# Attention keys split once per head, and the low half of the logits multiplied over 64 partitions

## The chip, the cores and the metric

The kernel runs on one core of one Trainium2 chip. The metric is the device time of one execution in microseconds, lower is better. Several runs were timed; one further execution was profiled.

## The reference

A two-layer encoder. Each layer projects the normed input (512 positions, 1024 channels), runs a differential attention of 4 heads beside a long-convolution branch, gates both and projects back. The part that the change touches, cut to what is computed:

```python
q, k: (B, S=512, ATTN_HEADS=4, 2, ATTN_QK_DIM=64)
logits = jnp.einsum('bhcqd,bhckd->bhcqk', q_blk, kt)          # contraction over 64
p = jax.nn.softmax(logits + bias[None, :, None], axis=-1)
w = p[:, :, 0] - lam * p[:, :, 1]                              # two components per head
o = jnp.einsum('bhqk,bhkd->bhqd', w, vt)
```

So every head has two components c = 0, 1, each with 64 key and query channels, and every block of 128 query rows needs one 128 x 512 logits product per component.

## The kernel before, in words

All products are made of two-part numbers: a value is split into a rounded high part and the remainder (`split`, L207 on ScalarE and L208 on VectorE), and a product is high x high + high x low + low x high, three matmuls (`mm3`, L192). Weights come in by DMA as `wraw`, are split into `whi` and `wlo`, and a dense projection of 128 channels is 24 matmuls of 128 x 128 x 512 into a PSUM tile `pd`.

One layer is a long list of steps. In the stretch around the change, `layer` mixes three lists: the 16 attention row blocks (4 heads x 4 blocks, `head_rows`, `head_av`, `head_out`), the dense projections of the next head or of the convolution branch, and in layer 0 also pieces of the filter computation. `mix` spreads them evenly; the tile scheduler then orders the instructions of each engine by priority and its own readiness estimate, so an edit in one step can shift others. In the trace the stretch with the logits lies from about 60 to 182 us (layer 0) and from 555 to 655 us (layer 1).

For one head, `head_proj` has steps q, k and z. Step q (L602, L603) builds two tiles, one per component: the 64 rows of component c hold the high half of the queries, the other 64 rows hold the low half of the same queries. Step k (L607 to L615) builds for each component two key tiles of 128 rows. `kh` holds the high half of the component's 64 key rows, twice: on rows 0 to 63 and on rows 64 to 127 (two ScalarE copies, L612). `kl` holds the low half (VectorE, L614) on the component's own rows and zeros (GpSimd memset, L613) on the other rows. A head's two pairs take two buffers of the pool `s1`.

`head_rows` then does per component two matmuls at L640, both with the same stationary operand, the 128-row query tile. The first, against `kh`, gives (q high + q low) x k high in one pass; the second, against `kl`, gives q high x k low, with the q low rows meeting zeros. VectorE adds the position bias and takes the row extreme (L643), ScalarE takes the exponential (L645), and VectorE combines the components (L650, L651). `head_av` transposes the weights (L659), and `head_out` multiplies by the values (L192 into `po`).

Of the kernel before, what the change touches and what calls it, by code (L numbers as in the profile page):

```python
# [10 lines left out]
F32 = mybir.dt.float32  # L11
F32R = mybir.dt.float32r
AF = mybir.ActivationFunctionType
ALU = mybir.AluOpType
# [108 lines left out]
def tiles(t):  # L123

    return t.rearrange("p (a c) -> p a c", a=4)
# [9 lines left out]
def ahead(n):  # L135

    def wrap(f):
        def g(self, *args):
            with self.tc.high_priority(offset=n):
                return f(self, *args)  # L140
        return g
    return wrap
# [3 lines left out]
class Net:  # L146
# [442 lines left out]
    def head_proj(self, l, h):  # L589


        nc = self.nc
        st = {}

        def q():
            ps = self.proj(l, QC + h * P)
            st["q"] = self.two_of("s1", F32R)
            for c in range(2):
                r, n = slice(c * 64, c * 64 + 64), slice(64 - c * 64, 128 - c * 64)
                q2 = st["q"][c]  # L600
                hi, lo, src = tiles(q2[r]), tiles(q2[n]), tiles(ps[r])[:, :, ::-1]
                nc.scalar.activation(out=hi, in_=src, func=AF.Copy, scale=-0.125)  # L602
                nc.vector.scalar_tensor_tensor(out=lo, in0=src, scalar=-0.125, in1=hi.bitcast(F32), op0=ALU.mult, op1=ALU.subtract)  # L603

        def k():
            ps = self.proj(l, KC + h * P)
            st["k"] = []  # L607
            for c in range(2):
                r, n = slice(c * 64, c * 64 + 64), slice(64 - c * 64, 128 - c * 64)
                kh, kl = self.two_of("s1", F32R)  # L610
                for d in (r, n):
                    nc.scalar.copy(out=kh[d], in_=ps[r])  # L612
                nc.gpsimd.memset(kl[n].bitcast(F32), 0.0)  # L613
                nc.vector.tensor_tensor(out=kl[r], in0=ps[r], in1=kh[r].bitcast(F32), op=ALU.subtract)  # L614
                st["k"].append((kh, kl))  # L615

        def z():
            ps = self.proj(l, ZAC + h * P)
            st["za"] = self.t("za")
            self.silu2(ps, st["za"])  # L620

        return st, [q, k, z]

    @ahead(20)
    def head_rows(self, l, h, i, st):


        nc = self.nc
        if i == 0:
            st["B"] = self.t("ld")  # L630
            t = self.tab[h:h + 1, :]
            self.load(st["B"][:, :896], bass.AP(tensor=t.tensor, offset=t.offset + 1, ap=[[1, P], [1, 896]]))
            st["s"] = self.small(8, "s")
        tsl = slice(i * P, (i + 1) * P)
        s0, s1 = (st["s"][:, 4 * c + i:4 * c + i + 1] for c in range(2))
        p = []
        for c in range(2):
            ps = self.ps("pq")
            for n in range(2):
                nc.tensor.matmul(ps, lhsT=st["q"][c][:, tsl], rhs=st["k"][c][n], start=(n == 0), stop=(n == 1))  # L640
            lg = self.t("a")
            m = self.small(1, f"m{c}")
            nc.vector.tensor_tensor_reduce(out=lg, in0=ps, in1=st["B"][:, 384 - i * P:896 - i * P], scale=1.0, scalar=3e38,  # L643
                                           op0=ALU.add, op1=ALU.min, accum_out=m)
            nc.scalar.activation(out=lg, in_=lg, func=AF.Exp, scale=-1.0, bias=m, accum_out=(s0, s1)[c])  # L645
            p.append(lg)
        r = self.small(1, "r")
        nc.vector.reciprocal(out=r, in_=s1)
        n1 = self.small(1, "n1")
        nc.vector.scalar_tensor_tensor(out=n1, in0=r, scalar=self.nlam[:, l:l + 1], in1=s0, op0=ALU.mult, op1=ALU.mult)  # L650
        nc.vector.scalar_tensor_tensor(out=p[0], in0=p[1], scalar=n1, in1=p[0], op0=ALU.mult, op1=ALU.add)  # L651
        st[i] = p[0]
# [434 lines left out]
```

## Time and profile before

| | |
|---|---|
| median of 3 runs | 963.67 us (961.45 to 964.77) |
| the profiled execution, its own time | 964.15 us |
| span of that execution, first to last instruction | 962.3 us |
| TensorE busy in it | 917.5 us (95%) |
| VectorE, ScalarE, GpSimd busy | 733.4 us (76%), 467.8 us (49%), 39.5 us (4%) |
| mean granted TensorE clock | 0.991 of full speed |

The profile separates TensorE into PE (matmuls) and PEld (loads of the stationary operand, which overlap matmuls). A matmul's recorded end is modelled and overlaps the next one's start, so the distance from start to start is what a matmul costs in a stream, not its recorded duration.

### The profile page before, as it was taken

The page shows a single profiled execution, that of the slowest core. Times are in us where ns is not written, and L with a number is a line of the kernel's source. Part 1 is how long each engine was busy: PE and PEld are TensorE (multiplying, and loading weights), DVE is VectorE, ACT ScalarE, POOL GpSimd, SP SyncE. Part 2 cuts the span into 40 slices and gives each one's busy share as a digit, 9 for nine tenths or more (in the row PEclk, how much of TensorE's full clock was granted, in tenths as well). Part 3 has the DMA queues.
Part 4 walks back from the last instruction along what each step waited for, and adds up shares of the span by engine and source line. Part 5 has one row for each costly group of instructions (what it writes and reads, how often), then busy time and mean ns, then how long its engine had stood idle before and what let it go on. Part 6 is the DMA issues. An engine that isn't in the chain of part 4 may idle for free.

```text
span 962.3 us, 13082 instructions
## 1 busy us (share of the span) xinstructions
PE 917.5 (95%) x4563; PEld 762.0 (79%) x4563; DVE 733.4 (76%) x1415; ACT 467.8 (49%) x889; POOL 39.5 (4%) x58
## 2 busy tenths in 40 slices
PE   5999998999999989999999999999999998999996
PEld 4777777888788878887787878888888887888885
DVE  5679889889889878888647478886788988854623
ACT  5467766554444333565444366664443532333521
POOL 2000000001000000000002000000000000000000
PEclk9999999999999999999999999999999999999999
DMA  6532342443543434244654322333333634233512
GB/s 218 152 115 60 105 129 84 144 122 88 153 120 109 134 109 131 77 145 130 218 176 151 87 81 80 96 89 119 100 107 103 197 112 130 67 98 99 166 53 89
DMA packets 141544, 114.12 MB, mean 119 GB/s; under 512 B 7106, under 2 KB 122464, under 8 KB 141477
## 3 DMA queue, kind: packets, MB, share of 16 engines
q1 hardware_dynamic: 140901, 111.31, 38.7%
q0 software_dynamic: 576, 1.97, 0.7%
q8 instruction: 36, 0.59, 0.3%
q14 instruction: 31, 0.25, 0.1%
HBM read 98.26 MB, written 14.99 MB: 118 GB/s over the span
## 4 chain that ended last, share of the span: by engine, by line
PE 42%; DVE 6%; DMA 2%; ACT 1%; POOL 1%; issue 0%; DVEq 0%; POOLq 0%; ACTq 0%; SPq 0%
PE pd L192 29%; PE po L192 4%; PE pq L192 4%; DMA wraw<-in_w_in 2%; PE pq L640 2%; PE po L204 1%; PE pq L204 1%; PE pt L659 1%; DVE s L961 1%; DVE cx L825 1%; DVE cx L828 0%; DVE yh L936 0%; DVE ld L961 0%; DVE cx L829 0%; POOL rout L226 0%
## 5 line engine op out<-in xcount | busy, mean ns | idle before, releaser
L192 PE MATMUL pd<-hT,whi 128*128 128x512 f32 x1408 | 453.0, 395 | 4.6 <-ACT a L889 2.6
L192 PEld LDWEIGHTS pd<-hT,whi 128*128 128x128 f32 x1408 | 260.7, 188 | 57.5 <-ACT a L889 3.4
L192 PE MATMUL pd<-hT,wlo 128*128 128x512 f32 x704 | 277.6, 394 | 1.9 <-DVE wlo L208 1.8
L207 ACT CAST whi<-wraw 128x512 fp32r<-128x512 f32 x216 | 133.8, 620 | 225.8 <-PE pd L192 116.4
L208 DVE TENSOR_TENSOR wlo<-wraw,whi 128x512 fp32r<-128x512 f32 x216 | 146.4, 687 | 63.7 <-ACT whi L207 62.9
L192 PEld LDWEIGHTS pd<-hT,wlo 128*128 128x128 f32 x704 | 132.4, 188 | 29.7 <-DVE wlo L208 3.1
L645 ACT ACTIVATE a<-a,m 128x512 f32<-128x512 f32 x64 | 46.1, 721 | 20.7 <-DVE m L643 20.4
L643 DVE CUSTOM_DVE_ANT_0 a<-pq,ld 128x512 f32<-128x512 f32 x64 | 43.3, 686 | 4.1 <-PE pq L640 3.3
L640 PE MATMUL pq<-s,s 128*128 128x512 f32 x128 | 46.3, 408 | 0.1
L192 PE MATMUL pd<-ya,whi 128*128 128x512 f32 x128 | 41.7, 393 | 0.0
L724 DVE SCALAR_TENSOR_TENSOR u<-pd,vec,u 128x256 f32<-128x256 f32 (+2 forms) x80 | 39.2, 530 | 2.5 <-ACT u L722 2.3
L192 PE MATMUL pd<-yh,whi 128*128 128x512 f32 x128 | 39.8, 390 | 0.0
L204 PE MATMUL po<-s,fh 128*128 128x256 f32 x160 | 32.4, 302 | 4.4 <-ACT s L207 2.0
L207 ACT CAST s<-cx 128x1024 fp32r<-128x1024 f32 x24 | 25.2, 1050 | 22.9 <-DVE cx L834 20.3
L204 PE MATMUL pq<-s,fh 128*128 128x256 f32 x160 | 35.2, 291 | 0.0
L204 PEld LDWEIGHTS po<-s,fh 128*128 128x128 f32 x160 | 26.9, 206 | 6.8 <-ACT s L207 2.9
L192 PE MATMUL po<-s,yh 128*128 128x256 f32 x192 | 29.3, 287 | 2.1 <-DVE n L650 1.4
L192 PEld LDWEIGHTS po<-s,yh 128*128 128x128 f32 x192 | 26.4, 191 | 5.4 <-ACT s L207 2.1
L208 DVE TENSOR_TENSOR s<-cx,s 128x1024 fp32r<-128x1024 f32 x24 | 29.3, 1222 | 0.6 <-ACT s L207 0.5
L204 PEld LDWEIGHTS pq<-s,fh 128*128 128x128 f32 x160 | 26.8, 189 | 3.2 <-DVE b L437 0.9
L640 PEld LDWEIGHTS pq<-s,s 128*128 128x128 f32 x128 | 23.6, 193 | 5.3 <-issue 0.9
L192 PEld LDWEIGHTS pd<-yh,whi 128*128 128x128 f32 x128 | 23.9, 188 | 4.8
(240 smaller groups left out, 1563.3 us busy)
## 6 DMA issues: line engine op xcount, KB each, us to landing
wraw<-in_w_in SPq DMA_DIRECT2D x192, 256.0 KB
H<-b SPq DMA_DIRECT2D x40, 256.0 KB
ld<-H SPq DMA_DIRECT2D x16, 512.0 KB
wraw<-in_w_out SPq DMA_DIRECT2D x32, 256.0 KB
wraw<-in_w_pa SPq DMA_DIRECT2D x16, 256.0 KB
wraw<-in_w_ph SPq DMA_DIRECT2D x16, 256.0 KB
ld<-tab SPq DMA_DIRECT2D x8, 448.0 KB
yh<-in_x SPq DMA_DIRECT2D x4, 512.0 KB
```

Of the source, the lines that this page charges most:

```text
L192: self.nc.tensor.matmul(out, lhsT=l, rhs=r, start=(first and i == 0), stop=(last and i == n - 1))
L204: self.nc.tensor.matmul(out, lhsT=b, rhs=y, start=(i == 0), stop=(i == len(ops) - 1))
L207: self.nc.scalar.copy(out=hi, in_=src)
L208: self.nc.vector.tensor_tensor(out=lo, in0=src, in1=hi.bitcast(F32), op=ALU.subtract)
L640: nc.tensor.matmul(ps, lhsT=st["q"][c][:, tsl], rhs=st["k"][c][n], start=(n == 0), stop=(n == 1))
L643: nc.vector.tensor_tensor_reduce(out=lg, in0=ps, in1=st["B"][:, 384 - i * P:896 - i * P], scale=1.0, scalar=3e38, op0=ALU.add, op1=ALU.min ...
L645: nc.scalar.activation(out=lg, in_=lg, func=AF.Exp, scale=-1.0, bias=m, accum_out=(s0, s1)[c])
L659: nc.tensor.transpose(out=ps[:, k], in_=w[:, k * P:(k + 1) * P], identity=self.ident)
L724: nc.vector.scalar_tensor_tensor(out=o, in0=src, scalar=w[j], in1=o, op0=ALU.mult, op1=ALU.add)
L825: nc.vector.tensor_tensor(out=X[:, 2 * s:2 * s + 2], in0=U[0], in1=odd, op=op)
L961: nc.vector.scalar_tensor_tensor(out=xt[:, cs], in0=st["o"][tt][:, cs], scalar=r, in1=xt[:, cs], op0=ALU.mult, op1=ALU.add)
```

## The change

In step k, one `split` over all 128 partitions makes the high half (`both`) and the low half (`kl`) of both components at once; the two memsets and the two 64-row subtractions go. `both` is only used to form `kl`; the doubled high tiles are still copied from PSUM, 4 copies of 64 rows, into one more buffer, so that a head again takes two buffers for its keys. In `head_rows` the second matmul of a component takes only the component's own 64 rows of the query tile and of `kl`.

```diff
         def k():
             ps = self.proj(l, KC + h * P)
-            st["k"] = []
+            both, kl = self.two_of("s1", F32R)
+            self.split(both, kl, ps)
+            kh = self.two_of("s1", F32R)
             for c in range(2):
-                r, n = slice(c * 64, c * 64 + 64), slice(64 - c * 64, 128 - c * 64)
-                kh, kl = self.two_of("s1", F32R)
-                for d in (r, n):
-                    nc.scalar.copy(out=kh[d], in_=ps[r])
-                nc.gpsimd.memset(kl[n].bitcast(F32), 0.0)
-                nc.vector.tensor_tensor(out=kl[r], in0=ps[r], in1=kh[r].bitcast(F32), op=ALU.subtract)
-                st["k"].append((kh, kl))
+                r = slice(c * 64, c * 64 + 64)
+                for d in range(2):
+                    nc.scalar.copy(out=kh[c][d * 64:d * 64 + 64], in_=ps[r])
+            st["k"] = kh, kl
...
-            for n in range(2):
-                nc.tensor.matmul(ps, lhsT=st["q"][c][:, tsl], rhs=st["k"][c][n], start=(n == 0), stop=(n == 1))
+            kh, kl = st["k"]
+            r = slice(c * 64, c * 64 + 64)
+            nc.tensor.matmul(ps, lhsT=st["q"][c][:, tsl], rhs=kh[c], start=True, stop=False)
+            nc.tensor.matmul(ps, lhsT=st["q"][c][r, tsl], rhs=kl[r], start=False, stop=True)
```

The change also moves instructions. On TensorE, at the second row block of the first head of layer 1, the row order before was as follows. L640 is the logits product (`s_5580` the queries, `s_5622` and `s_5627` the key tiles of the two components), L192 the dense projection beside it.

```order
L640 MATMUL pq<-s_5622,s_5580 128x512
L192 MATMUL pd<-hT,wlo 128x512
L640 MATMUL pq<-s_5622,s_5580 128x512
L192 MATMUL pd<-hT,whi 128x512 x2
L192 MATMUL pd<-hT,wlo 128x512
L640 MATMUL pq<-s_5627,s_5580 128x512
L192 MATMUL pd<-hT,whi 128x512
L640 MATMUL pq<-s_5627,s_5580 128x512
```

At the same place the order now is this one, with L640 the 128-row product (`s_5617` the two high tiles), L641 the 64-row one (`s_5614` the common low tile) and `s_5572` the queries.

```order
L640 MATMUL pq<-s_5617,s_5572 128x512
L192 MATMUL pd<-hT,wlo 128x512
L641 MATMUL pq<-s_5614,s_5572 128x512
L192 MATMUL pd<-hT,whi 128x512 x2
L192 MATMUL pd<-hT,wlo 128x512
L640 MATMUL pq<-s_5617,s_5572 128x512
L192 MATMUL pd<-hT,whi 128x512
L641 MATMUL pq<-s_5614,s_5572 128x512
```

Nothing moved here; each 64-row product simply stands between two 128-row ones. Over the whole program there are 64 L641, none of them next to another.

On ScalarE, in step k of that same head, the rows before were these (`s_5580` again the queries):

```order
L602 ACTIVATE s_5580<-pd 64x512 x2
L207 CAST whi<-wraw 128x512 x2
L612 CAST s_5622<-pd 64x512 x2
L612 CAST s_5627<-pd 64x512 x2
L207 CAST whi<-wraw 128x512
L645 ACTIVATE a,s<-a,m_5679 128x512
```

and now they are these, where line numbers from the logits on are one higher:

```order
L602 ACTIVATE s_5572<-pd 64x512 x2
L207 CAST whi<-wraw 128x512 x2
L207 CAST s_5614<-pd 128x512
L613 CAST s_5617<-pd 64x512 x4
L207 CAST whi<-wraw 128x512
L646 ACTIVATE a,s<-a,m_5669 128x512
```

One 128-row copy has come in ahead of the four 64-row copies. In layer 0, where the filter pieces are mixed in, the order of all engines shifts more widely; in layer 1 it stays close to what it was.

## Rows read from the trace of the kernel before

**Rows 1.** The page's busy time, share of span and instructions of each engine.
```profile
PE 917.5 (95%) x4563; PEld 762.0 (79%) x4563; DVE 733.4 (76%) x1415; ACT 467.8 (49%) x889; POOL 39.5 (4%) x58
```

**Rows 2.** Busy time of each engine in the two stretches with the logits.
```profile
core 0: us, PE busy (x) PEld busy (x) DVE busy (x) ACT busy (x) POOL busy (x), PEclk, DMA share, GB/s
55.00:183.00 128.00, 120.46 (x615) 97.74 (x614) 112.14 (x259) 86.86 (x177) 6.53 (x9) 0.99 0.34 100
...
555.00:656.00 101.00, 100.92 (x517) 84.91 (x517) 81.17 (x185) 64.95 (x137) 5.64 (x7) 1.00 0.29 85
```

**Rows 3.** Pieces of the chain that ended last: start, us, engine, line, matmuls.
```profile
475.87 5.44 PE po L192 x24
...
647.84 2.05 PE pd L192 x9
```

**Rows 4.** Both products of the logits, L640: ns min/median/max, first and last start.
```profile
L640 PEld LDWEIGHTS pq<-s,s x128: 186/188/338, 59.9 to 655.0; 128*128 128x128 f32 x128
L640 PE MATMUL pq<-s,s x128: 387/391/775, 60.2 to 655.2; 128*128 128x512 f32 x128
```

**Rows 5.** PE around the one product over 33 rows: start, us, shapes, count.
```profile
29.16 0.40 PE L192 MATMUL pd<-wlo,hT 128*128 128x512 f32 x1
29.48 1.12 PE L349 MATMUL pq<-u 33*128 33x512 f32 x2
30.54 0.73 PE L192 MATMUL pd<-whi,hT 128*128 128x512 f32 x2
31.11 0.40 PE L192 MATMUL pd<-wlo,hT 128*128 128x512 f32 x1
```

**Rows 6.** Weight loads at the same place, in brackets the idle time before.
```profile
28.93 0.19 PEld L192 LDWEIGHTS pd<-wlo,hT 128*128 128x128 f32 x1
29.48 0.29 PEld L349 LDWEIGHTS pq<-u 33*128 33x128 f32 x2 [0.36 <-issue]
30.53 0.30 PEld L192 LDWEIGHTS pd<-whi,hT 128*128 128x128 f32 x2 [0.76 <-DVE hT L208]
```

**Rows 7.** PE around the products over 32 rows and 4 columns.
```profile
53.83 0.39 PE L192 MATMUL pd<-hT,wlo 128*128 128x512 f32 x1
54.15 1.88 PE L309 MATMUL pt<-s,rb 32*4 32x512 f32 x4
55.95 0.73 PE L192 MATMUL pd<-hT,whi 128*128 128x512 f32 x2
56.52 0.40 PE L192 MATMUL pd<-hT,wlo 128*128 128x512 f32 x1
```

**Rows 8.** PE around the same kind of product as rows 5, over 128 rows.
```profile
58.13 0.39 PE L192 MATMUL pd<-hT,whi 128*128 128x512 f32 x1
58.36 1.04 PE L349 MATMUL pq<-u 128*128 128x512 f32 x2
58.84 0.79 PE L192 MATMUL pd<-hT,whi 128*128 128x512 f32 x1
59.47 0.39 PE L192 MATMUL pd<-hT,wlo 128*128 128x512 f32 x1
```

**Rows 9.** PE around a product with 128 rows and 4 columns.
```profile
117.84 0.39 PE L192 MATMUL pd<-hT,wlo 128*128 128x512 f32 x1
118.07 0.27 PE L698 MATMUL po<-ident,ro 128*4 128x128 f32 x1
118.18 0.38 PE L659 MATMUL pt<-ident,a 128*128 128x128 f32 x2
```

**Rows 10.** The instructions of step k: ns min/median/max, first and last start.
```profile
L612 ACT CAST s<-pd x32: 566/581/587, 54.7 to 627.3; 64x512 fp32r<-64x512 f32 x32
L613 POOL MEMSET s<- x16: 518/522/530, 22.0 to 605.9; 64x512 f32 x16
L614 DVE TENSOR_TENSOR s<-pd,s x16: 674/688/696, 56.0 to 628.0; 64x512 fp32r<-64x512 f32 x16
```

**Rows 11.** Splits of 128 rows on ScalarE and VectorE, from the page's costliest groups.
```profile
L207 ACT CAST whi<-wraw 128x512 fp32r<-128x512 f32 x216 | 133.8, 620 | 225.8 <-PE pd L192 116.4
L208 DVE TENSOR_TENSOR wlo<-wraw,whi 128x512 fp32r<-128x512 f32 x216 | 146.4, 687 | 63.7 <-ACT whi L207 62.9
```

**Rows 12.** Weight loads of the first row block of layer 1.
```profile
555.12 0.19 PEld L640 LDWEIGHTS pq<-s,s 128*128 128x128 f32 x1 [0.34 <-ACT s L612]
...
555.90 0.19 PEld L640 LDWEIGHTS pq<-s,s 128*128 128x128 f32 x1 [0.48 <-issue]
```

## The prediction

> **What bounds the kernel now.** I read the busy time of the engines first, then the two stretches that hold the logits, then the chain that ended last, and then single instructions. Over the span TensorE is busy 95% and no other engine over 76% [rows 1]. In layer 1's attention stretch it is busy 100.92 of 101 us; in layer 0's 120.46 of 128 us, and there VectorE has 112.14 us of work as well [rows 2]. So layer 1 is bound by TensorE alone, and layer 0 by TensorE with some waits. The chain of waits, which reaches back to 456 us and so covers layer 1, says the same: in the attention stretch it is made of pieces of dense matmuls [rows 3].
>
> Recorded matmul durations overlap, so I price by starts. 24 products of 512 columns took 5.44 us, 0.227 us each; inside the attention stretch 9 took 2.05 us, 0.228 us each [rows 3]. Both products of the logits run over 128 rows today, 128 of them, median record 391 ns with a 188 ns weight load [rows 4]: that is the ordinary dense record, and in the stream each costs 0.227 us. Half of them, 64, become 64-row products.
>
> **The change part by part.**
>
> *The 64-row product itself.* It still streams 512 columns. A product over 33 rows took no shorter stream than one over 128: its second pass left TensorE after 30.53 - 30.01 = 0.52 us, with the wait described next in it [rows 5, 6], where the 128-row passes stand 0.45 us apart (58.36 + 1.04 - 0.59, the record of one pass, is 58.81) [rows 8]. So leaving the zeros out saves no stream time: 0 us.
>
> *The switch between 128 and 64 rows.* The trace has one place where a product with fewer rows stands between dense ones, L349's first call, over 33 rows (the nearest to 64 that the trace has). In a dense stream the next weight load begins while the running matmul streams. Here it did not. The dense matmul before it started at 29.16 and its weights were loaded by 28.93 + 0.19 = 29.12, but the load for the 33 rows began only at 29.48, after 0.36 us of idle that no recorded wait explains [rows 6]. So the way in cost 29.48 - 29.16 = 0.32 us where 0.227 is usual: 0.09. The two passes then stand 1.12 - 0.59 = 0.53 us apart [rows 5] where a pass streams 0.43 us (four passes of L309 start over 1.88 - 0.59 = 1.29 us, [rows 7]): 0.10 of weight load that nothing hides. On the way out the dense load starts 0.52 us after the last pass (30.01 to 30.53), 0.09 over its stream; and the second dense matmul after it follows at 30.54 + 0.73 - 0.39 = 30.88, 0.34 us after the first where 0.227 is usual: 0.11 of load again in the open. Sum: 0.09 + 0.10 + 0.09 + 0.11 = 0.39 us for one excursion. As a check of the whole: from 29.16 to 31.11 are 1.95 us; undisturbed, one dense, two passes and two dense would take 0.227 + 2 x 0.43 + 2 x 0.227 = 1.54 us. Difference 0.41. I take 0.40.
>
> Is it the row count that costs, or the other number format of these products? The same line over 128 rows answers: from 58.13 to 59.47 are 1.34 us for one dense, two passes and one dense, which is 0.227 + 0.86 + 0.227 = 1.31 [rows 8]: almost nothing. Nor do few columns cost: a 128-row product of 4 columns starts 0.23 us after the dense one and is followed 0.11 us later [rows 9]. The second case with few rows, 32 rows by 4 columns, costs 56.52 - 53.83 = 2.69 us against 0.227 + 4 x 0.43 + 2 x 0.227 = 2.40: 0.29, the same less the load, which is short for 4 columns [rows 7]. That first load may hold a wait of its own, so I use this row as support only.
>
> The order now has 64 such products, each between 128-row ones, so 64 excursions: 64 x 0.40 = 25.6 us, 12.8 in each layer. The Trainium skill, "TensorEngine Tiling (Array Packing)", Tiling Modes, Key Properties, has a rule that speaks against this change: a change of tiling mode (not merely of tile) drains TensorE. The rows agree with it, and show more: by the drain alone, 0.09 in and 0.09 out, the sum would be 64 x 0.18 = 11.5 us; with the exposed loads it is 25.6.
>
> Bounds of this cost: below, nothing, if 64-row products of this format slip in as the 4-column one did [rows 9]; above, if the recorded end (0.39) and the whole load (0.19) have to pass each way [rows 4], 2 x (0.39 + 0.19) - 2 x 0.227 = 0.71 us, 64 x 0.71 = 45 us. I take 0.40, since the rows nearest in kind, half-height products in a dense stream, say so from both ends of the excursion.
>
> *How much of it shows.* In layer 1 TensorE has 0.08 us of idle in 101 [rows 2], so all 12.8 us. In layer 0 it has 7.5 us in 128, behind VectorE and ScalarE results, and while it is held up these catch up; VectorE at 112 of 128 us is itself close to the bound. I let a third of the 12.8 disappear there, 4.3 us, leaving 8.5. That third is a choice; its bounds are none and the idle 7.5.
>
> *Step k.* VectorE: two subtractions of 64 rows at 688 ns become one of 128 rows, and rows do not matter to it (687 ns at 128) [rows 10, 11]: 0.69 us saved per head, 5.5 us over 8 heads. VectorE is not the bound in layer 1; in layer 0 it may be partly: I count 0.5 us. ScalarE gets one 128-row copy of about 0.62 us more per head [rows 11], 5 us over the program, hidden in an engine busy 87 of 128 and 65 of 101 us [rows 2]; without that cover the first logits of a head would come 0.6 us later, 4.8 us in all. The order puts the copy first, so the four high tiles come later by that much, with the exponentials and weight splits behind them; the dense products cover it. The GpSimd memsets (16 x 522 ns, [rows 10]) go; GpSimd is busy 4% and nothing waited for L613: 0 us. Layer 1's first row block waits today for step k, 0.34 + 0.48 us at the first component [rows 12]; the new order starts these products later in the dense stream, worth at most about 1 us; I take 0.5. No DMA is added, though in layer 0 a few issues on SyncE's queue change places by a position or two: 0, give or take 3 us.
>
> **Sum.** 12.8 + 8.5 - 0.5 - 0.5 = 20.3 us. On the profiled execution's own 964.15 us (span 962.3 and 1.85 around it) that is 984.5; that execution lies 0.5 us above the median of 963.67, on which it is 984.0. I predict 984.
>
> **The rivals.** 0.3% of the time, 2.9 us, is about what a measurement here can tell from no change.
>
> *Smaller price.* The drains are paid and the loads hide, or layer 0 absorbs nearly all of its share: 11.5 us less up to 6, so 969 to 975. For it: 0.29 rather than 0.40 in the second place [rows 7]. Against: the exposed 0.10 and 0.11 in the first [rows 5].
>
> *Full price and more.* Layer 0 hides nothing (12.8 each, 989), or the price goes towards 0.71 (up to 1009). For it: the change puts one dense pass of 0.227 us between two switches, shorter than the two and four passes of 0.43 us in [rows 5, 7], and a row block's softmax starts later with each. Against: the price there sits at the switch and not in the stream's length.
>
> *No switch price, and faster: the other side.* If TensorE takes half-height products of this format like the 4-column one [rows 9], what remains is VectorE's 5.5 us and the 1 us of layer 1's first block. The time is then set in layer 0's stretch by VectorE, and it ends between 957 and 964. It decides where an excursion costs less than about 0.05 us (3 us in all). Against it stand both places with few rows. Half-height products running beside each other in the two halves of the array would also make it faster: 32 pairs at 0.227 us are 7 us, 957 again; but no L641 stands next to another in the order, and the rows show no overlap. The same page of the Trainium skill states, in the same list, that different tiles can load and multiply in parallel; no run here shows it.
>
> **Chances.** My forecast (975 to 989) 0.66; full price and more (989 to 1009) 0.13; smaller price (969 to 975) 0.11; no price 0.09 (0.06 within 0.3%, 0.03 faster); side by side 0.01. That is slower 0.90, same 0.06, faster 0.04. The range of 969 to 996 leaves out the last two cases and the upper half of the second, some 0.16. The forecast's own range is 975 to 989.
>
> **What would show it.** After the change, a weight load of L641 should begin 0.32 us after the start of the matmul before it, and the load behind it about 0.43 us after the load for L641, each with idle time that no other engine explains; the start after an excursion should come about 0.86 us after the dense start before it, instead of 0.454. Layer 1's stretch from its first to its last logits should grow from 100 to about 113 us, layer 0's by 7 to 10, and matmul counts stay the same. If L641 follows and is followed at 0.23 us, the price was wrong; if it is there and layer 1 does not grow, the chain was read wrongly.

## The result, and the profile after

The changed kernel takes 986.45 us (median of 4 runs, 982.73 to 989.25) against 962.56 us for the kernel before on the same chip (4 runs). The ratio is 1.0237, 95% interval 1.0215 to 1.026: it is slower. The forecast was 984 us, 20.3 over before. The profiled execution took 987.11 us, its span 985.3 us, 23.0 more than before.

The excursion looks as the prediction drew it. Here is TensorE in the changed kernel around one of the 64 half-height products, first matmuls, then weight loads (start, us, engine, line, shapes; idle time before in brackets).

```profile
590.95 0.40 PE L640 MATMUL pq<-s,s 128*128 128x512 f32 x1
591.18 0.40 PE L192 MATMUL pd<-hT,whi 128*128 128x512 f32 x1
591.51 0.50 PE L641 MATMUL pq<-s,s 64*128 64x512 f32 x1
591.94 0.50 PE L192 MATMUL pd<-hT,wlo 128*128 128x512 f32 x1
592.28 0.63 PE L192 MATMUL pd<-hT,whi 128*128 128x512 f32 x2
```
```profile
590.95 0.19 PEld L192 LDWEIGHTS pd<-hT,whi 128*128 128x128 f32 x1
591.51 0.18 PEld L641 LDWEIGHTS pq<-s,s 64*128 64x128 f32 x1 [0.37 <-issue]
591.94 0.19 PEld L192 LDWEIGHTS pd<-hT,wlo 128*128 128x128 f32 x1 [0.24 <-issue]
592.05 0.42 PEld L192 LDWEIGHTS pd<-hT,whi 128*128 128x128 f32 x2
```

L640 and the dense product behind it start 0.23 us apart. The load for L641 then begins 0.33 us after the dense start and not earlier, with 0.37 us of idle that no engine explains; the dense load behind it begins 0.43 us later; and the second dense product after the excursion stands 0.34 us behind the first. From 591.18 to 592.28 are 1.10 us where three dense starts take 0.68: about 0.4 us, as at the one 33-row place of the kernel before [rows 5, 6]. Over all 64 the median distances between starts are 0.32 us on the way in, 0.43 to the product behind, and 0.34 from there to the next; single ones differ where a neighbour is a smaller product or waits for another engine. The grouped view has 63 of the 64 loads waiting for nothing that the profile shows:

```profile
L641 PEld LDWEIGHTS pq<-s,s x64: 182/183/285, 60.2 to 679.4; 64*128 64x128 f32 x64
...
  issue: 19.6, 63
```

To see where the 23.0 us lie I cut the span at four points of TensorE's work that all kernels share: the last transpose of layer 0's norm, the last value product of layer 0's heads, the same two in layer 1, and the end. Each line below is such a stage (window, its length, busy time of each engine with counts, granted clock, DMA). Before:

```profile
28.00:196.00 168.00, 160.44 (x806) 129.16 (x805) 139.86 (x317) 106.30 (x215) 6.53 (x9) 0.99 0.37 108
196.00:531.00 335.00, 321.19 (x1626) 268.39 (x1625) 274.46 (x502) 156.41 (x289) 13.58 (x18) 0.99 0.44 132
531.00:671.00 140.00, 139.90 (x703) 117.10 (x702) 102.43 (x224) 81.89 (x169) 5.75 (x7) 1.00 0.31 91
671.00:963.00 292.00, 279.66 (x1366) 234.28 (x1365) 200.97 (x336) 108.98 (x189) 7.62 (x9) 0.99 0.37 110
```

After:

```profile
28.00:204.00 176.00, 172.18 (x801) 128.83 (x800) 137.81 (x313) 107.24 (x218) 4.73 (x4) 0.98 0.35 101
204.00:542.00 338.00, 322.07 (x1621) 268.83 (x1621) 274.30 (x502) 156.77 (x288) 13.41 (x14) 0.98 0.43 132
542.00:696.00 154.00, 153.77 (x712) 116.42 (x711) 101.11 (x221) 84.50 (x173) 3.98 (x3) 1.00 0.28 83
696.00:986.00 290.00, 277.48 (x1361) 232.13 (x1359) 200.45 (x336) 108.47 (x189) 7.47 (x9) 0.99 0.37 111
```

The windows are rounded to 1 us; with the marks' own start times (28.5, 196.3, 530.7, 671.4 before and 28.0, 203.7, 542.2, 695.8 after) the stages are:

| stage, us | before | after | difference | forecast |
|---|---|---|---|---|
| up to the norm of layer 0 | 28.5 | 28.0 | -0.5 | 0 |
| layer 0's heads | 167.8 | 175.7 | +7.9 | +8.0 |
| layer 0's convolutions to layer 1's norm | 334.4 | 338.5 | +4.1 | 0, give or take 3 |
| layer 1's heads | 140.7 | 153.6 | +12.9 | +12.3 |
| the rest | 290.9 | 289.5 | -1.4 | 0 |

One trace of each kernel stands behind these stages. Four of the kernels in this document (before, and three of the experiments) have the same order of instructions on every engine; what the edits leave alone varies among them from 332.4 to 335.3 us in the stage between the layers and from 288.6 to 291.7 in the last one. So the -1.4 us in the last line needs no cause in the change.

The stage rows show the kind of cost: in layer 1 the matmul's busy time grows from 139.90 to 153.77 us while the number of matmuls stays near 705, and the load's busy time stays at 117 us. TensorE does the same work with holes between. From its first to its last logits layer 1 takes 111.3 us (568.1 to 679.4), 11.2 more than before, where about 13 more were forecast, and layer 0 takes 130.8 us, 8.6 more, where 7 to 10 were.

### The profile page after: what moved, and what is told of

The parts are those of the page before. It is cut to its first block, busy times and chain, and to the rows that moved or that the text cites. A ratio compares the mean times of both kernels' runs of the same rounds, so it can differ in the third digit from the quotient of the medians.

```text
span 985.3 us, 13037 instructions
## 1 busy us (share of the span) xinstructions
PE 941.9 (96%) x4563; PEld 759.2 (77%) x4563; DVE 729.4 (74%) x1407; ACT 471.6 (48%) x897; POOL 34.0 (3%) x42
## 4 chain that ended last, share of the span: by engine, by line
PE 43%; DVE 6%; DMA 1%; ACT 1%; issue 0%; POOL 0%; DVEq 0%; POOLq 0%; ACTq 0%; SPq 0%
PE pd L192 30%; PE po L192 4%; PE pq L192 4%; PE pq L641 1%; PE po L204 1%; DMA wraw<-in_w_in 1%; PE pq L640 1%; PE pt L660 1%; PE pq L204 1%; DVE s L962 1%; DVE s L208 0%; DVE yh L937 0%; DMA wraw<-in_w_pa 0%; DVE ld L962 0%; DVE cx L835 0%
## 5 line engine op out<-in xcount | busy, mean ns | idle before, releaser
L192 PE MATMUL pd<-hT,whi 128*128 128x512 f32 x1408 | 459.1, 400 | 3.7 <-ACT a L890 2.6
L192 PEld LDWEIGHTS pd<-hT,whi 128*128 128x128 f32 x1408 | 262.2, 190 | 61.9 <-issue 8.2
L192 PE MATMUL pd<-hT,wlo 128*128 128x512 f32 x704 | 281.1, 399 | 4.1 <-DVE wlo L208 4.0
L192 PEld LDWEIGHTS pd<-hT,wlo 128*128 128x128 f32 x704 | 133.4, 189 | 34.0 <-DVE wlo L208 5.7
L192 PE MATMUL pd<-ya,whi 128*128 128x512 f32 x128 | 41.7, 393 | 0.0
L192 PE MATMUL pd<-yh,whi 128*128 128x512 f32 x128 | 39.9, 390 | 0.0
L204 PE MATMUL po<-s,fh 128*128 128x256 f32 x160 | 29.4, 282 | 3.5 <-ACT s L207 2.3
L641 PE MATMUL pq<-s,s 64*128 64x512 f32 x64 | 32.0, 500 | 0.0
L192 PE MATMUL po<-s,yh 128*128 128x256 f32 x192 | 31.4, 298 | 0.3 <-DVE rom L689 0.2
L192 PEld LDWEIGHTS po<-s,yh 128*128 128x128 f32 x192 | 26.0, 194 | 5.7 <-issue 3.6
L204 PEld LDWEIGHTS po<-s,fh 128*128 128x128 f32 x160 | 24.5, 188 | 5.9 <-ACT s L207 3.1
L723 ACT ACTIVATE u<-pd,vec 128x257 f32<-128x257 f32 (+2 forms) x40 | 22.6, 602 | 12.4 <-PE pd L192 12.4
L192 PEld LDWEIGHTS pd<-yh,whi 128*128 128x128 f32 x128 | 23.9, 188 | 4.8
```

Source lines behind the costliest of these rows:

```text
L192: self.nc.tensor.matmul(out, lhsT=l, rhs=r, start=(first and i == 0), stop=(last and i == n - 1))
L204: self.nc.tensor.matmul(out, lhsT=b, rhs=y, start=(i == 0), stop=(i == len(ops) - 1))
L641: nc.tensor.matmul(ps, lhsT=st["q"][c][r, tsl], rhs=kl[r], start=False, stop=True)
L723: nc.scalar.activation(out=o, in_=src, func=AF.Identity, scale=w[1], bias=b)
```

## The experiments

Ten kernels ran, in three groups, each with the kernel before on the same chip: its median was 962.07 us in the first group, 962.72 in the second and 961.89 in the third. "Layer 1's stage" below is the fourth line of the table, 140.7 us before.

**One half of the change alone: the 64 rows** (step k and the zeros as before).

```diff
-            for n in range(2):
-                nc.tensor.matmul(ps, lhsT=st["q"][c][:, tsl], rhs=st["k"][c][n], start=(n == 0), stop=(n == 1))
+            kh, kl = st["k"][c]
+            r = slice(c * 64, c * 64 + 64)
+            nc.tensor.matmul(ps, lhsT=st["q"][c][:, tsl], rhs=kh, start=True, stop=False)
+            nc.tensor.matmul(ps, lhsT=st["q"][c][r, tsl], rhs=kl[r], start=False, stop=True)
```


> The kernel before, with its step k and its zeros untouched; only the second product of the logits takes the component's own 64 rows. Theory (switch): each of the 64 half-height products costs 0.40 us more, 12 in layer 1 and 8 to 9 in layer 0, so 20 us over before: 978 to 988. Rival (the new step k or the order that came with it is what costs): nothing left here, 960 to 966.

Measured 984.67 us, ratio 1.0231 (1.02 to 1.0263). Layer 1's stage is 694.1 - 540.5 = 153.6 us, the changed kernel's figure. Layer 0's is 206.6 - 28.1 = 178.5 us, 10.7 over before. The order of instructions on every engine is that of the kernel before, so the half-height products carry the loss without any help from step k or from a new order.

**The other half alone: the split** (the changed kernel, second product over all rows).

```diff
-            nc.tensor.matmul(ps, lhsT=st["q"][c][r, tsl], rhs=kl[r], start=False, stop=True)
+            nc.tensor.matmul(ps, lhsT=st["q"][c][:, tsl], rhs=kl, start=False, stop=True)
```


> The changed kernel, its order of TensorE instructions row for row the same, but the second product runs over all 128 rows of the common low tile. Left out: the zeros, so the other component's low half is added to the logits. Theory (switch): the 21 us of the attention stretches go; a stall of about 4 us that the changed kernel has near 251 us, outside them, stays if it comes from the order: 962 to 968. Rival (step k or the order): stays at 980 or above.

Measured 962.56 us, ratio 1.0003 (0.9984 to 1.0021): the loss is gone, with the order of instructions on every engine that of the changed kernel. Left out are the zeros, so the other component's low half is added to the logits; this changes values and not the work. Its stages:

```profile
28.00:193.00 165.00, 159.07 (x805) 127.81 (x803) 136.71 (x313) 107.60 (x218) 4.73 (x4) 1.00 0.38 109
193.00:529.00 336.00, 321.13 (x1623) 268.24 (x1623) 274.35 (x502) 156.66 (x288) 13.41 (x14) 0.99 0.44 132
529.00:670.00 141.00, 140.29 (x709) 117.86 (x708) 99.58 (x221) 84.40 (x173) 3.03 (x3) 1.00 0.30 91
```

Against the changed kernel this isolates the row count. Layer 1's stage is 141.1 us, 12.5 less. Layer 0's is 164.4 us (28.4 to 192.8), 11.3 less than after and 3.4 less than before. So in layer 0 the stage is 11.3 us longer with the half-height products, and 3.4 shorter with the new step k and the order that came with it. The first kernel gives the same two differences on the other side: 10.7 us with the step k of before, and 178.5 - 175.7 = 2.8 between the two kernels with half-height products. A lower clock has a share in some of these (see below). The convolution stage, 336.2 us, keeps 1.8 of the 4.1 us.

**Fewer excursions: pairs.** The two 64-row products of a row block are issued behind its two 128-row ones; with the scheduler's order, 16 of 32 pairs ended up adjacent, 15 of them in layer 0.

```diff
+        banks = [self.ps("pq") for _ in range(2)]
+        high = [nc.tensor.matmul(banks[c], lhsT=st["q"][c][:, tsl], rhs=kh[c], start=True, stop=False) for c in range(2)]
+        for c in (1, 0):
+            r = slice(c * 64, c * 64 + 64)
+            low.append(nc.tensor.matmul(banks[c], lhsT=st["q"][c][r, tsl], rhs=kl[r], start=False, stop=True))
+        after(low[1], low[0])
```


> The changed kernel, with the two 64-row products of a row block issued after its two 128-row products; in the resulting order 16 of the 32 pairs stand directly next to each other, one on rows 64 to 127, one on rows 0 to 63, so 48 excursions in place of 64. Theory (switch): 16 x 0.40 = 6.4 us less than the changed kernel, near 980; if two half-height products in different halves also run side by side, the second of a pair starts right after the first and another 3 us go, 977. Rival (the price is the 64-row product's own, paid per product): 986, with 0.40 us also between the two of a pair.

Measured 980.11 us, ratio 1.0191 (1.0161 to 1.0221). That is 6.3 us under the changed kernel's median; the two were not run side by side, and the median does not separate 980 from 977. The trace does: in all 16 adjacent pairs the second product starts 3 to 4 ns after the first. One pair:

```profile
90.12 0.39 PE L640 MATMUL pq<-s,s 128*128 128x512 f32 x1
90.44 0.50 PE L644 MATMUL pq<-s,s 64*128 64x512 f32 x2
90.88 0.50 PE L192 MATMUL pd<-hT,wlo 128*128 128x512 f32 x1
```

Two products (x2) together take no longer than one record, 0.50 us, and the next dense product starts 0.44 us after the pair: the halves ran side by side.

**Fewer rows, but no half height: 96 rows** (the kernel before otherwise).

```diff
+            nc.tensor.matmul(ps, lhsT=st["q"][c][0:96, tsl], rhs=kl[0:96], start=False, stop=True)
```


> The kernel before, with the second product over rows 0 to 95 for both components. Left out: rows 96 to 127 of the low half of component 1. Theory (switch): what costs is the change to a half-height product, and 96 rows still need the full height, so 960 to 966 and starts 0.227 us apart. Rival (any product over fewer than 128 rows makes the next load wait): as with 64 rows, 978 to 988.

Measured 962.98 us, ratio 1.0007 (0.9987 to 1.0027). It is not a smaller row count that costs. The 96-row products stand in the ordinary stream:

```profile
587.62 0.39 PE L192 MATMUL pd<-hT,wlo 128*128 128x512 f32 x1
587.85 0.40 PE L641 MATMUL pq<-s,s 96*128 96x512 f32 x1
588.08 0.63 PE L192 MATMUL pd<-hT,whi 128*128 128x512 f32 x2
```

**64 rows in layer 1 only** (the kernel before otherwise).

```diff
+            r = slice(c * 64, c * 64 + 64) if l else slice(0, 128)
```


> The kernel before with the component's own 64 rows in the second product of layer 1 only; layer 0 as before. Theory (switch, nothing hidden in layer 1): 32 x 0.40 = 12.8 us over before, 974 to 976, all of it between the first and the last logits of layer 1. Rival (the softmax chain behind the later logits adds waits, or TensorE's prefetch hides some): 968 or less, or 980 and more.

Measured 972.86 us, ratio 1.0115 (1.0078 to 1.0152), a little under the 974 to 976 that I wrote. Layer 1's stage is 681.5 - 528.1 = 153.4 us, 12.7 more than before, and layer 0's is unchanged at 195.7 - 27.9 = 167.8. The missing 2 us lie in stages that the edit does not touch: 332.4 us between the layers against 334.4, with a granted clock of 1.00 there against 0.99.

**All 32 pairs adjacent** (as the pairs above, the half-height products at a somewhat higher priority).

```diff
+            with self.tc.high_priority(offset=5):
+                low.append(nc.tensor.matmul(banks[c], lhsT=st["q"][c][r, tsl], rhs=kl[r], start=False, stop=True))
```


> As e3_pairs, with all 32 pairs of 64-row products directly next to each other, on different halves of the rows. Theory (switch, and the halves run side by side): each pair costs 0.40 for the excursion and saves one product of 0.227, so 32 x 0.17 = 5.5 us over before: 966 to 970. Rival (side by side was an accident of the 16 pairs of layer 0): 32 x 0.40 = 12.8 over, 975.

**The same, both products on rows 0 to 63** (component 1 then multiplies rows of component 0).

```diff
-            r = slice(c * 64, c * 64 + 64)
+            r = slice(0, 64)
```


> As e6_all_pairs, but both products of a pair stand on rows 0 to 63. Computation changed: component 1 multiplies the wrong half. Theory: the second product starts 0.227 us after the first, not side by side, and still shares the excursion: 32 x 0.40 = 12.8 us over before, 973 to 977. Rival (a pair runs together whatever its rows): as e6_all_pairs, 966 to 970. Rival (the price is paid per product): 986.

Measured 970.22 us, ratio 1.0084 (1.0055 to 1.0113), on different halves, and 976.99 us, ratio 1.0136 (1.0091 to 1.0181), on the same half. The first median lies just above the band I gave, the second at its upper edge; the stages of layer 1 hit it: 677.2 - 533.7 = 143.5 us, 2.8 over before (16 x 0.17 = 2.7), and 685.7 - 538.4 = 147.3 us, 6.6 over before (16 x 0.40 = 6.4). The pair on different halves:

```profile
584.36 0.40 PE L640 MATMUL pq<-s,s 128*128 128x512 f32 x1
584.69 0.50 PE L645 MATMUL pq<-s,s 64*128 64x512 f32 x2
585.11 0.86 PE L192 MATMUL po<-s,yh 128*128 128x256 f32 x5
```

and on the same half:

```profile
584.64 0.40 PE L640 MATMUL pq<-s,s 128*128 128x512 f32 x1
584.97 0.73 PE L645 MATMUL pq<-s,s 64*128 64x512 f32 x2
585.63 0.50 PE L192 MATMUL pd<-hT,whi 128*128 128x512 f32 x1
```

The second product of this pair alone:

```profile
585.30 0.39 PE L645 MATMUL pq<-s,s 64*128 64x512 f32 x1
```

Both pairs begin 0.33 us after the product before. The one on different halves is left 0.42 us after its start, the other 0.66, one dense product (0.23) more. On the same half the second starts 0.33 us behind the first, not the 0.227 that I wrote, and the dense product 0.33 us behind the second. So the price belongs to the excursion, not to the product, and side by side needs different rows.

**Everything in halves.** Queries and keys are split once over 128 rows, nothing is doubled, and three half-height products per component alternate between the halves.

```diff
+        for n, (x, y) in enumerate(((qh, kh), (qh, kl), (ql, kh))):
+            for c in (1, 0):
+                r = slice(c * 64, c * 64 + 64)
+                with self.tc.high_priority(offset=0 if last is None else 5):
+                    m = nc.tensor.matmul(banks[c], lhsT=x[r, tsl], rhs=y[r], start=(n == 0), stop=(n == 2))
```


> No doubled tiles at all: queries and keys are split once over 128 rows, and the three products of each component run over its own 64 rows, the two components in turn on the two halves; per head 1 ScalarE copy and 1 VectorE subtraction for the queries and the same for the keys. In the resulting order 21 row blocks are one group of six, 10 are one and five, one is two and four. Theory (halves side by side, 0.227 per pair, 0.40 per excursion): 21 x 0.17 + 11 x 0.8 = 12 us over before, less 0 to 3 us of VectorE relief in layer 0: 970 to 976. Rival (in a longer group the loads get in the way and halves run one after the other): 31 us over, 993.

Measured 966.45 us, ratio 1.0044 (1.0025 to 1.0063): some 4 us better than the band. A longer group does keep the halves side by side; what I mis-sized is how much layer 0 gives back, where its stage is 195.2 - 27.9 = 167.3 us, 0.5 under before, with 27 excursions in it (5 row blocks in one group of six, 11 in two pieces).

**The same, every row block one group of six, and a mixture.** The first product of a row block waits for the readers of both PSUM banks; the mixture uses this in layer 0 and the form before in layer 1.

```diff
+                    for x_ in self.readers[-2:] if last is None else []:
+                        self.tc.add_manual_dep(m.ins, x_.ins.name, mybir.DependencyInfo(mybir.DependencyClass.Sync, mybir.DependencyReason.DATA))
```


> As e8_all_halves, but the first product of a row block waits until both PSUM banks are free, so that all 32 row blocks are one group of six; excursions 32 in place of 43. Theory (switch): 32 x 0.18 = 5.8 us over before for TensorE, less what the four instructions fewer per head on ScalarE and two on VectorE give back in layer 0 (e8 came out some 8 us below its own sum, part of it excursions that TensorE's waits there hid): 958 to 964. Rival (what e8 hid were its excursions, nothing else): 965 to 969, no gain over e8.

> Layer 0 as in e9_sixes, layer 1 as in the kernel before. Theory: layer 1 is bound by TensorE alone, so going back there to full-height products takes off its 16 x 0.18 = 2.9 us: 955 to 962, 3 us under e9_sixes. Rival (the plain split's fewer instructions count in layer 1 too): not under e9_sixes.

Measured 958.25 us, ratio 0.9958 (0.994 to 0.9976), and 958.27 us, ratio 0.9959 (0.9938 to 0.998): both beat the kernel before by 0.4%, and, by the medians of runs that were not side by side, the changed one by some 28 us. One group of six:

```profile
565.14 0.40 PE L193 MATMUL pd<-hT,wlo 128*128 128x512 f32 x1
565.47 0.96 PE L637 MATMUL pq<-s,s 64*128 64x512 f32 x6
566.36 0.72 PE L193 MATMUL pd<-hT,whi 128*128 128x512 f32 x2
566.92 0.40 PE L193 MATMUL pd<-hT,wlo 128*128 128x512 f32 x1
```

From 565.14 to 566.92 are 1.78 us; three dense products and the four full-height ones that the six replace would take 7 x 0.227 = 1.59. So a row block costs TensorE 0.19 more, and layer 1's stage is indeed 671.3 - 527.8 = 143.5 us, 2.8 over before. The gain is in layer 0: 189.9 - 28.4 = 161.5 us, 6.3 under before although TensorE has more to do there:

```profile
28.00:190.00 162.00, 160.18 (x840) 123.29 (x838) 134.50 (x310) 94.03 (x197) 3.60 (x4) 1.00 0.39 111
```

TensorE is busy in all but 1.8 of these 162 us; before, in all but 7.6 of 168. ScalarE has 12.3 us less to do and VectorE 5.4 less, and the granted clock is 1.00 against 0.99. Which of these, or the new order, brought the gain was not separated. The mixture has 668.0 - 526.8 = 141.2 us in layer 1, as planned, but its median is not lower: that a layer bound by TensorE should keep the full-height form is shown by the stage, not by the time.

## Why the prediction was right, point by point

**The bound.** Right. Layer 1's heads had no slack, and 32 excursions lengthened their stage by 12.9 us; with 64 rows in layer 1 alone the stage grew by 12.7. The 0.5 us that the sum took off for layer 1's first row block did not come: with the new step k the stage is 153.6 us against 153.6 at 64 rows, and 141.1 against 140.7 at 128. The waits in [rows 12] are those of weight loads, and TensorE's matmuls had only 0.08 us of idle time there to give back [rows 2].

**No gain from leaving the zeros out.** Right; the 96-row kernel costs what 128 rows cost, and two 64-row products on the same half start 0.33 us apart, not closer than the 0.227 of dense ones.

**The price of an excursion, 0.40 us.** Right in size, and in its parts: 0.33 on the way in, 0.43 to the next load, 0.34 behind it. It was read from a product of another format and 33 rows; the format and the exact row count did not matter. One of its readings held by luck. The 0.09 on the way out were taken for the switch, but [rows 6] name a VectorE split as what that load waited for, and the split ends at 28.80 + 1.73 = 30.53, where the load starts:

```profile
28.80 1.73 DVE L208 TENSOR_TENSOR hT<-pt,hT 128x256 fp32r<-128x256 f32 x4 [2.18 <-ACT hT L207]
```

So that place alone could not tell the two apart. The same-half pair shows a way out without such a wait: 0.33 us, 0.10 over a dense start. And the 0.86 us that the prediction named as a sign do not follow from its own terms: 0.32 in and 0.43 to the next load make 0.75 us from dense start to dense start, with 0.11 more behind the second; 0.76 were measured (591.18 to 591.94).

The rule that a change of tiling mode drains TensorE, in the Trainium skill, "TensorEngine Tiling (Array Packing)", Tiling Modes, Key Properties, agrees with these rows. By the rows the weight load in the open comes on top of it.

**How much of it shows in layer 0.** The total was right, 7.9 us against 8.0, by luck: its terms were not. The prediction let a third of 12.8 us vanish and counted 0.5 us for VectorE. The stages show 10.7 to 11.3 of the 12.8 us, and 2.8 to 3.4 us given back by the new step k with its order. Part of these differences is the clock: in layer 0's stage the granted clock was 0.99 before, 0.98 in the changed and in the 64-rows-only kernel, and 1.00 in the split-only one. The changed kernel has two stretches there in which TensorE ran at the lower of its two levels, 1.2 GHz:

```profile
134.60:138.00 3.40, 3.40 (x12) 2.43 (x12) 2.16 (x6) 1.80 (x5) 0.00 (x0) 0.50 0.22 80
175.50:179.00 3.50, 3.47 (x9) 2.75 (x9) 3.50 (x9) 1.83 (x4) 0.00 (x0) 0.51 0.51 150
```

In the second, dense products start 0.43 us apart instead of 0.227:

```profile
177.05 0.63 PE L192 MATMUL pd<-hT,wlo 128*128 128x512 f32 x1
177.47 1.06 PE L192 MATMUL pd<-hT,whi 128*128 128x512 f32 x2
178.33 0.63 PE L192 MATMUL pd<-hT,wlo 128*128 128x512 f32 x1
```

I estimate that each of the two costs at most 1.6 us: eight dense products fill it at 0.43 us, and at 0.227 they would take 1.8. The 64-rows-only kernel has one of twice that length (163.9 to 170.7), the kernel before one like these (157.0 to 160.4), the split-only kernel none. So up to 3.2 of the 11.3 us, 1.6 of the 10.7, and 1.6 of the 3.4 may be the clock's, and none of the 2.8. The first of the two stretches follows a wait of 1.81 us for ScalarE (at 132.64), the second no wait of that size; whether the excursions have a part in them was not tried. What is sure is that the new step k with its order gave back more than the 0.5 us, and that the half-height products cost more in the stage than the 8.5, so that two mis-sized terms cancelled; how much of the second is the clock stays open. Which part of the first is VectorE's saving and which the order was not separated.

**Step k.** The counts came as forecast (8 subtractions of 686 ns in place of 16; one ScalarE copy more per head, no memsets), and together with the order it moves the whole time by nothing that can be told (1.0003).

**The convolution stage.** The prediction gave the moved instructions nothing, give or take 3 us for DMA issues that change places; the stage is 4.1 us longer. Its longest stall is a matmul that waits 3.11 us for VectorE's weight split, and TensorE runs at a granted clock of 0.72 in the stretch around it. VectorE had itself waited for ScalarE's `yh`, and ScalarE for a weight DMA (the three waits, then the window, as above):

```profile
249.60 0.62 ACT L207 CAST whi<-wraw 128x512 fp32r<-128x512 f32 x1 [4.27 <-DMA wraw<-in_w_in]
251.68 1.29 DVE L208 TENSOR_TENSOR yh<-s,yh 128x512 fp32r<-128x512 f32 x2 [2.07 <-ACT yh L207]
254.76 0.79 PE L192 MATMUL pd<-hT,wlo 128*128 128x512 f32 x1 [3.11 <-DVE wlo L208]
```
```profile
250.00:262.00 12.00, 8.89 (x30) 7.03 (x29) 10.32 (x17) 4.99 (x9) 0.00 (x0) 0.72 0.32 95
```

Before, VectorE waited 0.83 us for the same `yh`; why the DMA lands later now was not followed. In the same kernel with full-height products the wait is 2.57 us, the stretch is at 0.86, and the stage keeps 1.8 of the 4.1 us. The 64-rows-only kernel, which has the order of before, needs 540.5 - 206.6 = 333.9 us. Over all runs the four kernels with that order lie between 332.4 and 335.3 us here, and the eight with a new step k in layer 0 at 335.7 to 340.3. So a part goes with the new step k and its order, though 1.8 us by itself is within the spread of one order. The other 2.3 us go with a longer stall and a longer time at the lower clock; what brings these out was not tried.

**The rivals.** "No switch price" fell with the first two kernels, "smaller price" and "full price" with the stages, though "full price" came near in layer 0: by the stages, clock included, it hid 1.5 to 2.1 of the 12.8 us. Side by side, which I gave 0.01 because no two half-height products were adjacent, did not occur in the changed kernel; made adjacent, it occurs.

## What to carry to other kernels

Before cutting a product down to half the rows, look at what stands next to it: between full-height products a half-height one cost 0.4 us here, nearly two products, and saved nothing, so zeros that fill up the rows were the cheaper choice. If half-height products are wanted, collect them and alternate the two halves, since one excursion then carries all of them and pairs run together. Price an edit per stage and check each term by a kernel that undoes it alone: in layer 0 two wrong terms gave a right sum. Look at the granted clock of both stages before a difference of one or two microseconds is given a cause.

## What the runs showed of the hardware

Two products over 64 rows on different halves of the rows start 3 to 4 ns apart, and so do their loads; on the same half the second starts 0.33 us behind the first. The Trainium skill, "TensorEngine Tiling (Array Packing)", says in Tiling Modes, Key Properties, that different tiles can load and multiply in parallel. These traces show it: the 32 pairs above, and the pairs in a group of six. A product over 96 rows between products over 128 rows costs nothing (0.23 us from start to start), one over 64 costs 0.40 us more. A stretch at the lower clock has dense products 0.43 us apart instead of 0.227.
